# Full-row operands for the compressed attention products, retention norms in pairs of heads, and the last down-projection block ordered by token tiles

## The chip, the cores and the metric

The kernel runs on one core of one Trainium2 chip. The metric is the device time of one execution in microseconds (us); lower is better. Work is spread over TensorE (PE in the profile; its weight loads are PEld), VectorE (DVE), ScalarE (ACT), GpSimd (POOL) and the DMA queue of SyncE (SP).

## What is computed

Two post-norm layers over 512 tokens of width 1024. Each layer projects the tokens to a pooling mixer, six retention heads and six sparse-attention heads (two key/value groups of three heads), maps their outputs back with `w_out`, normalizes, and runs a gated MLP of width 2816 with a causal convolution, then a second layer norm. The parts that matter here, cut from the reference:

```python
def _retention(q, k, v, g, gn_g, pos):          # 6 heads of 64
    ...
    o = (inner + cross).reshape(b, t, h, dh)
    mu = jnp.mean(o, axis=-1, keepdims=True)
    var = jnp.mean(jnp.square(o - mu), axis=-1, keepdims=True)
    on = ((o - mu) * lax.rsqrt(var + GN_EPS)).reshape(b, t, RET_WIDTH) * gn_g
    return (jax.nn.silu(g.astype(f32)) * on).astype(q.dtype)

def _compress(kv, pos_emb, w1, b1, w2):         # 31 blocks of 32 tokens, stride 16
    ...
    return jax.nn.gelu(flat @ w1 + b1) @ w2

    # in _nsa: scores, softmax and values over the 31 compressed blocks
    s_c = jnp.einsum('btgrd,bngd->bgrtn', qg, kc)
    p_c = _masked_softmax(s_c, ends[None, :] <= tq[:, None])
    o_cmp = jnp.einsum('bgrtn,bngd->btgrd', p_c, vc)

    # per layer
    x = _layernorm(DEEPNORM_ALPHA * x + mix, ln1_g[l], ln1_b[l])
    f = _conv_ffn(x, ffn_w_gate[l], ffn_w_up[l], ffn_conv_w[l], ffn_conv_b[l], ffn_w_down[l])
    x = _layernorm(DEEPNORM_ALPHA * x + f, ln2_g[l], ln2_b[l])
```

## The kernel before

Tokens are four tiles t of 128 (`NT`). float32 products are made from float32r parts: every operand is split into a rounded half and the rest (`hi_lo`: a copy on ACT, a subtraction on DVE), and `mm3` issues three matmuls, hi*hi, hi*lo and lo*hi. Where the left operand holds both halves side by side (`vcs`, `VS`, `VR`: 64 columns of hi and 64 of lo), one matmul per half of the right operand is issued and the two column halves are added afterwards.

The order of the work is not written by hand. `Plan.record` collects every instruction with its dependencies and a price (`price`); `Plan.schedule`, a list scheduler with one queue for each engine, picks by rank among instructions that are ready in its model, and also decides which buffers are given out. PSUM has eight banks with limits for each use (`BANKS`: at most 3 for "mm", 4 for "tr", 5 for "s", 1 for "pv"); 29 scratch tiles "u", 14 weight tiles "w" (`NW`, one 128x1024 half each) and 5 raw weight tiles. On each engine the issued order is then fixed. All instructions are recorded at line 424, so the trace is read by tiles.

In each layer: the retention stage (`retention`, with the projections, pooling, `fill_cmp_*` and `fill_kcs` as filler), the attention stage (`attention`: `scores` and `values` for each token tile i and group g, with the output projection and the first norm, `fill_out1`, as filler), then the MLP (`ff_plain`, `ff_seven`) and its down-projection.

- `retention`: for each head h, `o_part` accumulates [128, 512] in one "pv" bank, adds its halves into `otr` [64, 512] (ACT copy, DVE add); `n_part` transposes `otr` in four pieces of 64 rows, norms the head with DVE, ACT and a POOL `pow`, and writes half of `YB`; after every second head `t_part` transposes `YB` into `mixT`.
- The compressed branch: `fill_cmp_mlp` leaves `ab` (66 rows), which `fill_cmp_act` transposes; `fill_cmp_out` makes `kd` (64 rows) and `vcs` (32 rows); `fill_kcs` transposes `kd`. In `values(i, g)` the job with b == 2 is the compressed one: the probabilities `pc` [128, 3, 32] are transposed to 32 rows, split into `PT`, and multiplied with `vcs`, two matmuls of 32 rows and 384 columns among those of `VS` with 128 rows.
- The down-projection runs in blocks of features (`BLOCKS`, the last one of 6). `ffn_order` lists ("w", block, half h of 512 columns) and ("down", block, h, t). In the last block h = 0 comes first for all t (tiles 0 to 2 together in three banks, all but the last feature first), then the weights of h = 1, then h = 1 for each t. A token tile is normed (`layernorm`) right after its h = 1 part. In the last layer the norm has form "m" (`LAST_NORM`): ACT and POOL take columns 704 to 1024 (`SHARE`), DVE the rest; then SP stores the tile. In the first layer the tile is transposed for layer 2.

Of the kernel before, what the change touches and what calls it, by code (L numbers as in the profile page):

```python
# [426 lines left out]
def trunk(tc, x_d, pos_d, w_in, w_out, w_gate, w_up, w_down, cst_d, prm_d,  # L427
# [4 lines left out]
    with es:  # L432
# [424 lines left out]
        prm = C([P, L, Q_N], F, "prm")  # L857
        for l in range(L):
# [113 lines left out]
            vcs = C([32, 2, P], R, "vcs", 1)  # L972
# [21 lines left out]
            def fill_cmp_mlp(i):  # L994

                ch, cl = state.pop(("CT", i))
                W = take(2)
                q = ps("mm", [P, 512])[0:66, 0:256].rearrange("p (a n) -> p a n", a=2)
                for t in range(8):
                    w = W[t // 4]  # L1000
                    mm3(q, (ch[:, t], cl[:, t]), (w[:, 0, :, t % 4], w[:, 1, :, t % 4]), t == 0, t == 7)
                ab = Q([66, 2, P], F, "ab", 1)
                nc.scalar.copy(ab, q)
                state["ab", i] = ab
                yield

            def fill_cmp_act(i):
                ab = state.pop(("ab", i))
# [4 lines left out]
                nc.scalar.copy(hs, pt)  # L1013
# [15 lines left out]
            def fill_cmp_out(i):  # L1029
                ht = state.pop(("ch", i))  # L1030
                q2 = ps("mm", [P, 512])[0:64, 0:64]
                mm3(q2, (ht[:, 0], ht[:, 1]), (w2[:, 0, i], w2[:, 1, i]), True, True)
                if i == 0:
                    kd = state["kd"] = Q([64, 2, 64], F, "kd", 1)
                    rope(q2.unsqueeze(1), 64, 1, cos[0:64, NT], nsin[0:64, NT], [kd[:, 0:1]])
                    nc.gpsimd.tensor_copy(kd[:, 1], kd[:, 0])
                else:
                    for g in range(2):
                        nc.scalar.copy(vcs[:, g, 0:64], q2[32 * g:32 * g + 32])
                        nc.vector.tensor_tensor(vcs[:, g, 64:128], q2[32 * g:32 * g + 32], vcs[:, g, 0:64].bitcast(F), OP.subtract)  # L1040
                yield

            def fill_kcs():
                kd = state.pop("kd")
# [16 lines left out]
            def retention():  # L1061
# [49 lines left out]
                def n_part(h, tmp):  # L1111
                    p, e = h // 2, h % 2
# [5 lines left out]
                    m = small([P, 4, NT])  # L1118
                    ors = cst[:, K_ORS + h:K_ORS + 24:6].unsqueeze(2).to_broadcast([P, NT, 64])
                    nc.vector.tensor_tensor(a, pn, ors, OP.mult)  # L1120
                    nc.vector.tensor_reduce(m[:, 0], a, AX.X, OP.add)
                    nc.vector.tensor_scalar(m[:, 0], m[:, 0], 1.0 / 64, None, OP.mult)
                    nc.vector.tensor_tensor(a, a, m[:, 0].unsqueeze(2).to_broadcast([P, NT, 64]), OP.subtract)
# [3 lines left out]
                    nc.gpsimd.tensor_tensor(m[:, 2], m[:, 1], mhalf[:, 0:NT], OP.pow)  # L1127
                    nc.vector.tensor_tensor(a, a, m[:, 2].unsqueeze(2).to_broadcast([P, NT, 64]), OP.mult)
                    if e == 0:
                        cache["yb"] = U([P, NT, 2, 64], n="YB")  # L1130
                    yb = cache["yb"]
                    engine(WHO[3]).tensor_tensor(yb[:, :, e], a, VG[p][:, 1, :, 64 * e:64 * e + 64], OP.mult)
                    if e:
                        return yb
# [13 lines left out]
                def back():  # L1148
# [5 lines left out]
                    if tmp is not None:  # L1154
                        later.append((n_part, h, tmp))

                def norm():
                    f, h, tmp = later.pop(0)
                    yb = f(h, tmp)
                    if yb is not None:  # L1160
                        later.append((t_part, h // 2, yb))
# [94 lines left out]
            def values(i, g):  # L1256
# [13 lines left out]
                for at, (b, j) in enumerate(jobs):  # L1270
# [4 lines left out]
                    PT = U([P, 2, 3, P], R, n="PT")  # L1275
                    hi_lo(PT[0:n, 0], PT[0:n, 1], pt[0:n])
# [37 lines left out]
            def layernorm(t, y, g, b, how, cuts=(0, 512, D)):  # L1314
# [7 lines left out]
                if how in "am":  # L1322
                    nc.vector.scalar_tensor_tensor(mv[:, 4:5], mv[:, 0:1], -1.0, mv[:, 3:4], OP.mult, OP.mult)
                for lo, hi, who in ((SHARE, D, "a"), (0, 512, "v"), (512, SHARE, "v")) if how == "m" else ((0, 512, how), (512, D, how)):
# [58 lines left out]
            if l == 0:  # L1383
                masks()
            one, mask = masked
# [111 lines left out]
            xT2 = None  # L1497
            if PLAIN:
# [10 lines left out]
            for what, *of in ffn_order:  # L1509
                if what == "seven":  # L1510
                    ff_seven(of[0])
                elif what == "w":
# [6 lines left out]
                    wd = take(-(-nb // 2))  # L1519
                elif what == "down":  # L1520
# [3 lines left out]
                    if lastb and h == 0 and t < 3:  # L1524

                        if t == 0:
                            qs = [ps("mm", [P, 512]) for _ in range(3)]
                            for ks in (range(nb - 1), (nb - 1,)):
                                for i in range(3):
                                    sum_down(qs[i], wd, b0, nb, i, ks)  # L1530
                            for i in range(3):
                                add_down(qs[i], ib, i, 0, 512)
                        continue
                    for lo, hi in ((0, 256), (256, 512)) if end else ((0, 512),):
                        q = ps("mm", [P, hi - lo])
                        sum_down(q, wd, b0, nb, t, range(nb), lo, hi)
# [83 lines left out]
NORM1, NORM2, LAST_NORM = "maav", "vvvv", "mmmm"  # L1620
SHARE = 704
# [55 lines left out]
```

## Time and profile before

| | us |
|---|---|
| median of 3 runs | 1276.33 (1276.01 to 1276.76) |
| the profiled execution | 1275.91 |
| its span | 1274.1 |
| PE busy | 1256.3 (99%) |
| PE weight loads busy | 1126.1 (88%) |
| DVE busy | 1027.2 (81%) |
| ACT busy | 705.3 (55%) |
| POOL busy | 339.4 (27%) |

The span is the time between the first and the last recorded instruction; the 1.8 us between it and the execution's time lie around it. A matmul's recorded duration is modelled and overlaps its neighbours' (a 512-column matmul is given 0.39 us while the next one starts 0.23 us later), so PE's cost is read from starts, not from durations.

### The profile page before, as it was taken

To read this page: it belongs to the slowest core of one execution; us is meant where nothing else is said; L and a number is where in the kernel's file an instruction comes from. 1 tells how busy PE (TensorE), PEld (TensorE's weight loads), DVE (VectorE), ACT (ScalarE), POOL (GpSimd) and SP (SyncE) were. 2 spreads that over 40 slices of the span, in tenths; PEclk is the share of its full clock that TensorE was granted. 3 is DMA by queue.
4 is the path that set the end of the run, shared out by engine and by line. 5 is a ranking of instruction groups with operands and counts; after the bars stand their busy time and mean duration, and the time that the engine had idled before them with its cause. 6 is when DMAs were issued, how large, how long until landed. Compare 5 with 4: busy or idle time off the path is not lost.

```text
span 1274.1 us, 21523 instructions
## 1 busy us (share of the span) xinstructions
PE 1256.3 (99%) x8044; PEld 1126.1 (88%) x8044; DVE 1027.2 (81%) x1957; ACT 705.3 (55%) x1459; POOL 339.4 (27%) x256
## 2 busy tenths in 40 slices
PE   9999999999999999999999999999999999999996
PEld 6789898889999999999888898888899999999995
DVE  7868888697888988888786687777887888888876
ACT  5445567665555555555334455865764555655540
POOL 1132303333322322212122322133513223222023
PEclk9999999999999999999999999999999999999998
DMA  8331513101433433345342215221023333434321
GB/s 273 117 85 32 168 68 119 48 1 34 120 105 99 120 91 108 109 125 154 122 141 83 67 50 182 80 71 34 18 77 90 95 106 99 122 102 126 100 67 67
DMA packets 142601, 123.24 MB, mean 97 GB/s; under 512 B 6688, under 2 KB 116000, under 8 KB 142496
## 3 DMA queue, kind: packets, MB, share of 16 engines
q1 hardware_dynamic: 142496, 121.86, 31.7%
q8 instruction: 63, 1.03, 0.3%
q14 instruction: 42, 0.34, 0.1%
HBM read 117.65 MB, written 4.19 MB: 96 GB/s over the span
## 4 chain that ended last, share of the span: by engine, by line
PE 94%; DVE 3%; ACT 2%; issue 0%; POOL 0%; POOLq 0%; DVEq 0%; ACTq 0%
PE mm L424 47%; PE s L424 39%; PE tr L424 5%; PE pv L424 3%; DVE y L424 1%; ACT P L424 1%; ACT PT L424 0%; DVE w L424 0%; DVE xq L424 0%; ACT y L424 0%; ACT xq L424 0%; DVE ps L424 0%; POOL y L424 0%; ACT xf L424 0%; DVE sm L424 0%
## 5 line engine op out<-in xcount | busy, mean ns | idle before, releaser
L424 POOL TENSOR_TENSOR w<-raw,w 128x1024 fp32r<-128x1024 f32 (+3 forms) x116 | 232.1, 2003 | 630.1 <-ACT w L424 355.7
L424 ACT CAST w<-raw 128x512 fp32r<-128x512 f32 (+2 forms) x403 | 290.7, 742 | 196.7 <-PE s L424 123.2
L424 DVE TENSOR_TENSOR w<-raw,w 128x512 fp32r<-128x512 f32 (+3 forms) x288 | 234.0, 831 | 41.2 <-ACT w L424 36.1
L424 PE MATMUL mm<-w,hT 128*128 128x512 f32 (+1 forms) x1074 | 262.3, 391 | 0.0
L424 PE MATMUL s<-xq,w 128*128 128x256 f32 x1944 | 251.1, 281 | 0.2
L424 PEld LDWEIGHTS s<-xq,w 128*128 128x128 f32 x1944 | 243.1, 189 | 6.2 <-DVE xq L424 0.6
L424 PE MATMUL mm<-w,xT 128*128 128x512 f32 (+3 forms) x1152 | 239.9, 353 | 1.8 <-DVE w L424 1.5
L424 PE MATMUL s<-xs,w 128*128 128x256 f32 x1824 | 234.0, 281 | 0.0
L424 PEld LDWEIGHTS s<-xs,w 128*128 128x128 f32 x1824 | 226.0, 189 | 2.3
L424 PEld LDWEIGHTS mm<-w,hT 128*128 128x128 f32 x1074 | 193.6, 188 | 37.5
L424 PEld LDWEIGHTS mm<-w,xT 128*128 128x128 f32 x1152 | 190.1, 188 | 27.1 <-ACT xT L424 1.7
L424 DVE TENSOR_TENSOR raw<-raw,raw 128x512 f32<-128x512 f32 (+1 forms) x114 | 100.3, 880 | 6.4 <-DMA raw<-in_w_up 4.8
L424 DVE TENSOR_TENSOR y<-y,mm 128x512 f32<-128x512 f32 (+1 forms) x97 | 63.2, 673 | 22.4 <-PE mm L424 21.9
L424 ACT COPY pq<-s 128x256 f32<-128x256 f32 x152 | 55.2, 368 | 43.0 <-PE s L424 42.7
L424 PE MATMUL mm<-w,mixT 128*128 128x512 f32 x240 | 74.5, 415 | 1.1 <-DVE OM L424 1.1
L424 DVE SCALAR_TENSOR_TENSOR pq<-gu,prm,pq 128x511 f32<-128x511 f32 x76 | 66.7, 877 | 3.5 <-ACT pq L424 3.2
L424 POOL TENSOR_TENSOR sm<-sm,mhalf 128x1 f32<-128x1 f32 (+1 forms) x28 | 26.5, 947 | 123.5 <-DVE sm L424 123.5
L424 DVE TENSOR_TENSOR gu<-s,pq 128x256 f32<-128x256 f32 x76 | 30.8, 418 | 29.2 <-PE s L424 25.0
L424 DVE TENSOR_TENSOR PT<-tr,PT 128x384 fp32r<-128x384 f32 (+1 forms) x96 | 48.9, 543 | 6.6 <-ACT PT L424 5.8
L424 ACT ACTIVATE P<-s,sm 128x128 f32<-128x128 f32 (+3 forms) x96 | 49.3, 533 | 8.1 <-DVE sm L424 7.8
L424 ACT CAST PT<-tr 128x384 fp32r<-128x384 f32 (+1 forms) x96 | 42.0, 482 | 19.7 <-PE tr L424 19.1
L424 POOL TENSOR_SCALAR P<-P,sm 128x384 f32<-128x384 f32 (+3 forms) x40 | 24.4, 624 | 104.0 <-DVE sm L424 66.0
(195 smaller groups left out, 1699.9 us busy)
## 6 DMA issues: line engine op xcount, KB each, us to landing
raw<-in_w_gate SPq DMA_DIRECT2D x76, 256.0 KB, 3.5
raw<-in_w_up SPq DMA_DIRECT2D x76, 256.0 KB, 3.8
raw<-in_w_down SPq DMA_DIRECT2D x36, 512.0 KB, 3.8
raw<-in_w_in SPq DMA_DIRECT2D x32, 512.0 KB, 4.3
raw<-in_w_out SPq DMA_DIRECT2D x14, 512.0 KB, 4.0
raw<-in_w_in SPq DMA_DIRECT2D x8, 530.0 KB, 4.3
raw<-in_w_down SPq DMA_DIRECT2D x16, 256.0 KB, 2.8
raw<-in_w_in SPq DMA_DIRECT2D x8, 384.0 KB, 3.2
```

Source lines behind the costliest of these rows:

```text
L424: getattr(getattr(self.nc, op.engine), op.method)(*a, **k)
```

## The change

Four edits:

1. `vcs`, `ab`, `kd` and two new tiles `ptc[g]` become constant tiles of 128 rows, zeroed once in `zeros()` (three ACT copies and three POOL memsets in the first layer). `vcs` holds its 32 rows twice; `ptc` holds the hi half of the transposed probabilities in rows 0 to 31 and the rest in rows 32 to 63. The compressed product of one (i, g) is one matmul over 128 rows. The transposes of `ab` and `kd` take 128 rows.
2. `o_part` writes two heads into one `otr` tile of 128 rows, `n_part` runs once for each pair: four transposes of 128 rows, and DVE, ACT and POOL instructions of 512 instead of 256 columns.
3. In the last block of the down-projection both weight halves are taken first; then (t, h) runs (0,0), (1,0), (0,1) together, then (1,1), (2,0), (2,1), (3,0), (3,1). A tile is normed after its h = 1 part.
4. The norm of the very last tile has form "e": as "m", with the columns from 832 (`LAST_SHARE`) for ACT and POOL.

The diff, cut to its core:

```diff
-            for h in range(2):
-                down.append(("w", b0, nb, h))
-                down.extend(("down", ib, b0, nb, h, t) for t in range(NT))
+            if b0 + nb < NFF:
+                for h in range(2):
+                    down.append(("w", b0, nb, h))
+                    down.extend(("down", ib, b0, nb, h, t) for t in range(NT))
+            else:
+                down.extend(("w", b0, nb, h) for h in range(2))
+                down.extend(("down", ib, b0, nb, h, t) for t, h in ((0, 0), (1, 0), (0, 1), (1, 1), (2, 0), (2, 1), (3, 0), (3, 1)))
...
+        vcs = C([P, 2, P], R, "vcs")
+        ptc = [C([P, 3, P], R, f"ptc{g}") for g in range(2)]
+        ab = C([P, 2, P], F, "ab")
+        kd = C([P, 2, 64], F, "kd")
+        def zeros():
+            z = U([P, 2 * P], n="z")
+            nc.gpsimd.memset(z, 0.0)
+            nc.scalar.copy(vcs, z.rearrange("p (a n) -> p a n", a=2))
+            for g in range(2):
+                nc.scalar.copy(ptc[g], z[:, 0:P].unsqueeze(1).to_broadcast([P, 3, P]))
+            nc.gpsimd.memset(ab, 0.0)
+            nc.gpsimd.memset(kd, 0.0)
...
-                pt = ps("tr", [P, 2, 66])
+                pt = ps("tr", [P, 2, P])
                 for a in range(2):
-                    tr(pt[:, a], ab[:, a], 66)
+                    tr(pt[:, a], ab[:, a])
...
+                    nc.scalar.copy(vcs[32:64], vcs[0:32].bitcast(F))
...
-                pt = ps("tr", [P, 64])
-                tr(pt, kd.rearrange("p a d -> p (a d)"), 64)
+                pt = ps("tr", [P, P])
+                tr(pt, kd.rearrange("p a d -> p (a d)"))
...
-                        tmp = U([64, 2, S], n="otr")
-                        nc.scalar.copy(tmp[:, 0], o[64:128])
-                        nc.vector.tensor_tensor(tmp[:, 1], o[0:64], tmp[:, 0], OP.add)
-                        return tmp
+                        e = h % 2
+                        if e == 0:
+                            cache["ot"] = U([P, 2, S], n="otr")
+                        tmp = cache["ot"]
+                        nc.scalar.copy(tmp[0:64, 0], o[64:128])
+                        nc.vector.tensor_tensor(tmp[64 * e:64 * e + 64, 1], o[0:64], tmp[0:64, 0], OP.add)
+                        return tmp if e else None
...
-                    pn = ps("tr", [P, NT, 64])
+                    pn = ps("tr", [P, NT, 2, 64])
                     for t in range(NT):
-                        tr(pn[:, t], tmp[:, 1, t * P:(t + 1) * P], 64)
-                    on = U([P, 2, NT, 64], n="on")
+                        tr(pn[:, t].rearrange("p e d -> p (e d)"), tmp[:, 1, t * P:(t + 1) * P])
+                    on = U([P, 2, NT, 2, 64], n="on")
...
+                    if n < P:
+                        mm(o, lhs, PT, first, last)
+                        return
                     mm(o, lhs, PT[0:n, 0], first, False)
                     mm(o, lhs, PT[0:n, 1], False, last)
...
-                    PT = U([P, 2, 3, P], R, n="PT")
-                    hi_lo(PT[0:n, 0], PT[0:n, 1], pt[0:n])
+                    if n < P:
+                        PT = ptc[g]
+                        hi_lo(PT[0:n], PT[n:2 * n], pt[0:n])
...
-                    if lastb and h == 0 and t < 3:
+                    early = ((0, 0), (1, 0), (0, 1))
+                    if lastb and (t, h) in early:
...
-NORM1, NORM2, LAST_NORM = "maav", "vvvv", "mmmm"
-SHARE = 704
+NORM1, NORM2, LAST_NORM = "maav", "vvvv", "mmme"
+SHARE, LAST_SHARE = 704, 832
```

## Rows read from the trace of the kernel before

**Rows 1.** Page: busy time by engine, and the chain that ended last by engine.

```profile
PE 1256.3 (99%) x8044; PEld 1126.1 (88%) x8044; DVE 1027.2 (81%) x1957; ACT 705.3 (55%) x1459; POOL 339.4 (27%) x256
...
PE 94%; DVE 3%; ACT 2%; issue 0%; POOL 0%; POOLq 0%; DVEq 0%; ACTq 0%
```

**Rows 2.** By stretch: length, busy us of PE, PEld, DVE, ACT, POOL, clock, DMA.

```profile
176.00:302.00 126.00, 124.14 (x736) 106.14 (x735) 97.68 (x219) 84.84 (x200) 44.95 (x42) 1.00 0.17 51
1266.00:1270.00 4.00, 0.00 (x0) 0.00 (x0) 2.66 (x5) 0.65 (x1) 2.88 (x5) 0.51 0.42 165
...
256.00:276.00 20.00, 20.00 (x114) 16.55 (x113) 18.88 (x43) 11.04 (x27) 5.29 (x7) 1.00 0.01 2
```

**Rows 3.** Timeline of PE, 128-row matmuls and transposes: start, us, what, shapes, count.

```profile
173.89 0.68 PE L424 MATMUL mm<-w,xT 128*128 128x384 f32 x3
...
607.61 21.79 PE L424 MATMUL mm<-w,hT 128*128 128x512 f32 x93
...
98.13 0.60 PE L424 MATMUL tr<-ident,YB 128*128 128x128 f32 x4
98.49 0.48 PE L424 MATMUL mm<-w,xT 128*128 128x256 f32 x2
```

**Rows 4.** Timeline of PE around one pair of compressed products, first layer.

```profile
245.07 0.95 PE L424 MATMUL mm<-w,mixT 128*128 128x512 f32 x3
245.94 0.43 PE L424 MATMUL pv<-PT,vcs 32*128 32x384 f32 x1
246.31 0.49 PE L424 MATMUL mm<-w,mixT 128*128 128x512 f32 x1
246.73 0.44 PE L424 MATMUL pv<-PT,vcs 32*128 32x384 f32 x1
247.10 0.51 PE L424 MATMUL mm<-w,mixT 128*128 128x512 f32 x1
```

**Rows 5.** Timeline of PE around another pair, back to back, first layer.

```profile
277.88 0.59 PE L424 MATMUL pv<-PT,VS 128*128 128x384 f32 x2
278.40 1.00 PE L424 MATMUL pv<-PT,vcs 32*128 32x384 f32 x2
279.33 0.44 PE L424 MATMUL pv<-PT,VS 128*128 128x384 f32 x1
```

**Rows 6.** Timeline of PE around the 64-row transposes of one retention head.

```profile
69.03 0.40 PE L424 MATMUL mm<-w,xT 128*128 128x512 f32 x1
69.36 0.46 PE L424 MATMUL tr<-ident,otr 64*128 64x64 f32 x4
69.75 0.39 PE L424 MATMUL s<-QTr,KSr 128*128 128x256 f32 x1
```

**Rows 7.** Chain that ended last, end of the attention stage, first layer.

```profile
273.08 1.51 ACT PT L424 x4
```

**Rows 8.** Groups by shape of DVE, a retention norm step: count, busy, mean ns, idle before.

```profile
L424 DVE TENSOR_TENSOR on<-on,sm 128x256 f32<-128x256 f32 x24 | 10.5, 437 | 1.0 <-POOL sm L424 0.8
```

**Rows 9.** Timeline of the end: last matmuls, norms of tiles 2 and 3.

```profile
1231.51 30.91 PE L424 MATMUL mm<-w,hT 128*128 128x512 f32 x150
...
1262.45 0.42 DVE L424 TENSOR_TENSOR y<-y,mm 128x256 f32<-128x256 f32 x1 [0.21 <-PE mm L424]
1262.79 0.15 DVE L424 TENSOR_SCALAR sm<-sm 128x1 f32<-128x1 f32 x1
...
1263.52 0.42 DVE L424 BATCH_NORM_STATS2 sm<-y 128x6 f32<-128x256 f32 x1
...
1264.36 0.65 ACT L424 ACTIVATE y<-y,sm 128x320 f32<-128x320 f32 x1 [4.74 <-DVE sm L424]
...
1268.88 0.94 POOL L424 TENSOR_TENSOR y<-y,lng 128x320 f32<-128x320 f32 x1 [0.96 <-ACT y L424]
1269.89 0.86 POOL L424 TENSOR_TENSOR y<-y,lnb 128x320 f32<-128x320 f32 x1
```

**Rows 10.** Timeline: layer 2's weights and first products; weights of the last block.

```profile
616.66 1.05 ACT L424 CAST w<-raw 128x1024 fp32r<-128x1024 f32 x1 [4.23 <-PE mm L424]
...
637.97 1.32 PE L424 MATMUL mm<-w,xT 128*128 128x512 f32 x5
...
1223.94 8.03 POOL L424 TENSOR_TENSOR w<-raw,w 128x1024 fp32r<-128x1024 f32 x3 [37.45 <-ACT w L424]
```

More of the change, by code (lines that the diff above doesn't have):

```diff
@@ L1033, in fill_cmp_out @@
                 if i == 0:
-                    kd = state["kd"] = Q([64, 2, 64], F, "kd", 1)
-                    rope(q2.unsqueeze(1), 64, 1, cos[0:64, NT], nsin[0:64, NT], [kd[:, 0:1]])
-                    nc.gpsimd.tensor_copy(kd[:, 1], kd[:, 0])
+                    rope(q2.unsqueeze(1), 64, 1, cos[0:64, NT], nsin[0:64, NT], [kd[0:64, 0:1]])
+                    nc.gpsimd.tensor_copy(kd[0:64, 1], kd[0:64, 0])
                 else:
                     for g in range(2):
-                        nc.scalar.copy(vcs[:, g, 0:64], q2[32 * g:32 * g + 32])
-                        nc.vector.tensor_tensor(vcs[:, g, 64:128], q2[32 * g:32 * g + 32], vcs[:, g, 0:64].bitcast(F), OP.subtract)
+                        v = vcs[0:32, g]
+                        nc.scalar.copy(v[:, 0:64], q2[32 * g:32 * g + 32])
+                        nc.vector.tensor_tensor(v[:, 64:128], q2[32 * g:32 * g + 32], v[:, 0:64].bitcast(F), OP.subtract)
+                    nc.scalar.copy(vcs[32:64], vcs[0:32].bitcast(F))
                 yield
             def fill_kcs():
-                kd = state.pop("kd")
-                pt = ps("tr", [P, 64])
-                tr(pt, kd.rearrange("p a d -> p (a d)"), 64)
+                pt = ps("tr", [P, P])
+                tr(pt, kd.rearrange("p a d -> p (a d)"))
+                pt = pt[:, 0:64]
                 nc.scalar.copy(kcs, pt)
@@ L1126, in n_part @@
                     nc.vector.tensor_scalar(m[:, 1], m[:, 1], 1.0 / 64, EPS, OP.mult, OP.add)
[L1127 to L1134, printed above, removed]
+                    nc.gpsimd.tensor_tensor(m[:, 0].rearrange("p t e -> p (t e)"), m[:, 1].rearrange("p t e -> p (t e)"), mhalf, OP.pow)
+                    nc.vector.tensor_tensor(a, a, each(m[:, 0]), OP.mult)
+                    yb = U([P, NT, 2, 64], n="YB")
+                    engine(WHO[3]).tensor_tensor(yb.rearrange("p t e d -> p t (e d)"), a.rearrange("p t e d -> p t (e d)"), VG[p][:, 1], OP.mult)
+                    return yb
                 def t_part(p, yb):
@@ L1154, in back @@
                     if tmp is not None:
-                        later.append((n_part, h, tmp))
+                        later.append((n_part, h // 2, tmp))
                 def norm():
-                    f, h, tmp = later.pop(0)
-                    yb = f(h, tmp)
+                    f, p, tmp = later.pop(0)
+                    yb = f(p, tmp)
                     if yb is not None:
-                        later.append((t_part, h // 2, yb))
+                        later.append((t_part, p, yb))
                 nxt_h = heads(0)
@@ L1384, in trunk @@
                 masks()
+                zeros()
             one, mask = masked
@@ L1497, in trunk @@
             xT2 = None
+            wd = [None, None]
             if PLAIN:
@@ L1518, in trunk @@
                             x_src = nc.tile(dp, [S, D], F, "xs", nm("xs"), 1)
-                    wd = take(-(-nb // 2))
+                    wd[h] = take(-(-nb // 2))
                 elif what == "down":
@@ L1523, in trunk @@
                     end = lastb and h == 1 and t == NT - 1 and l == L - 1
-                    if lastb and h == 0 and t < 3:
-                        if t == 0:
-                            qs = [ps("mm", [P, 512]) for _ in range(3)]
+                    early = ((0, 0), (1, 0), (0, 1))
+                    if lastb and (t, h) in early:
+                        if (t, h) == early[0]:
+                            qs = [ps("mm", [P, 512]) for _ in early]
                             for ks in (range(nb - 1), (nb - 1,)):
[L1529 to L1534, printed above, removed]
+                                for q, (i, j) in zip(qs, early):
+                                    sum_down(q, wd[j], b0, nb, i, ks)
+                            for q, (i, j) in zip(qs, early):
+                                add_down(q, ib, i, 512 * j, 512 * j + 512)
+                        if h == 0:
+                            continue
+                        done = True
+                    else:
+                        done = False
+                    for lo, hi in () if done else ((0, 256), (256, 512)) if end else ((0, 512),):
                         q = ps("mm", [P, hi - lo])
-                        sum_down(q, wd, b0, nb, t, range(nb), lo, hi)
+                        sum_down(q, wd[h], b0, nb, t, range(nb), lo, hi)
                         add_down(q, ib, t, 512 * h + lo, 512 * h + hi)
```

28 lines of the change are left out of this document (14 added, 14 removed).

## Prediction

> **What bounds the kernel now.** I read the page first: PE is busy in 99% of the span and makes 94% of the chain that ended last [rows 1]. DVE is next with 81%. So time taken off PE's stream is time gained, unless PE then waits for another engine. Busy time by stretch comes next: in the first layer's attention stage PE is busy for 124.1 of 126.0 us, DVE for 97.7 and ACT for 84.8 [rows 2]; DVE has room there except in one stretch of 20 us, where it is busy for 18.9. [...]
>
> A recorded matmul duration overlaps the next one, so the price of a matmul is the distance of two starts. In a run of 93 full-row matmuls of 512 columns this is (21.79 - 0.39) / 92 = 0.233 us, in one of three with 384 columns (0.68 - 0.34) / 2 = 0.17 us; four full-row transposes and the step to the next matmul take 98.49 - 98.13 = 0.36 us [rows 3]. (The 0.39 and 0.34 are what one such matmul is recorded with.) Against these I hold the matmuls with fewer rows.
>
> **Part 1, compressed products.** The third matmul of the first row starts about 245.62 (two steps of 0.233 and one late step of 0.085 before it). The 32-row product starts at 245.94, so 0.32 after a step of 0.233: 0.09 lost going in. It takes 246.31 - 245.94 = 0.37 until the full-row matmul starts, instead of 0.17: 0.20 lost coming out. The second product loses 246.73 - 246.31 - 0.233 = 0.19 going in and 0.20 coming out [rows 3, 4]. Together 0.68 us, and as one of the two products disappears, 0.17 more: 0.85 us for this pair. Another pair stands back to back [rows 5]: 279.33 - 278.40 = 0.93 for both, 0.10 before them (278.40 minus the second start near 278.13, minus 0.17), 1.03 in all; one full-row product of 0.17 remains: 0.86, of which some is a wait. The least a pair loses, without any wait, is 2 x 0.20 + 2 x 0.09 + 0.17 = 0.75. I take 0.78, near the low end since waits stay. There are 16 pairs (two layers, four token tiles, two groups): 16 x 0.78 = 12.5 us, bounds 12.0 and 13.8.
>
> [...]
>
> What is new beside it: zeroing, three ACT copies and three POOL memsets once, and one ACT copy per layer to double `vcs`. None feeds PE soon; estimate, from the 0.65 us of a 320-column ACT instruction [rows 9], under 2 us of ACT in a stage where no product of `vcs` is due yet: nothing on the path; if that cover were gone, 2 us. `ptc[g]` is written again only after the other group and a whole token tile, so its new wait is long satisfied. The split of `PT` keeps its instructions and their columns.
>
> **Part 2, retention in pairs.** A head's four 64-row transposes come in at 69.36 - 69.03 = 0.33 after a 512-column matmul (0.10 over 0.233) and take 69.75 - 69.36 = 0.39 to the next one [rows 6]: 0.49, for a pair of heads 0.98. One pair of 128-row transposes is 0.36 [rows 3]. Saved: 0.62 x 6 pairs = 3.7 us; without waits in the 0.39 perhaps 3.1. The two transposes of `kd` lose a way in and out in the same manner, 0.2 each, 0.4 together. Those of `ab` (66 rows, 66 columns) become 128 columns wide: 8 of them, at most 0.11 each at the pace of full transposes (0.36 for four, less the short last step), I take +0.2; a gain there has no source.
>
> The norm's DVE steps become half as many of twice the length. A 256-column step has 0.437 us [rows 8]; two of them 0.87, one of 512 columns between 0.44 and 0.87. DVE cannot lose by it, and five such steps on six pairs give it up to 6 x 5 x 0.43 = 13 us, more likely half. That lies beside PE and counts nothing. What grows is a pair's latency, by at most five steps of 0.43 on DVE and as much again on ACT and POOL, some 3 to 4 us. `mixT` of the last pair is not needed before the attention stage's filler, so nobody on PE waits; what is queued behind on DVE is the splitting of scores, each behind one step longer by at most 0.43.
>
> **Does PE's gain arrive?** The compressed products lie in the attention stage. Near its end the chain leaves PE: ACT's `PT` copies carry 1.5 us at 273 [rows 7], inside the stretch in which DVE is also nearly full [rows 2]. A product saved there turns into a wait. These are the last token tile's two pairs in each layer: 4 x 0.78 = 3.1 us. I write off 2.5 (bounds 0 and 6, the latter if the tile before is caught too). PE: 12.5 + 3.7 + 0.4 - 0.2 - 2.5 = 13.9 us.
>
> **Parts 3 and 4, the end.** PE's last matmul ends at 1262.4 and the span at 1274.1. DVE adds the last product at 1262.45 and then still works on tile 2 (its variance at 1262.79), so that tile 3's statistics start only at 1263.52 and its last POOL step ends at 1269.89 + 0.86 = 1270.75; store and end take 3.35 [rows 9]. After the change tile 2 has its last product two products of 18 matmuls earlier, 2 x 18 x 0.233 = 8.4 us, and is done. Tile 3 alone: add to 1262.87, statistics (0.42) and their sum to about 1263.56; from a variance to ACT 1264.36 - 1262.79 = 1.57, so ACT at 1265.13. ACT on 192 instead of 320 columns: 0.65 becomes 0.54; the two POOL steps 0.94 and 0.86 become at most that and, shrunk by the columns, at least 0.56 and 0.52; I take 0.73 and 0.71. With three gaps of 0.07 the end is 1265.13 + 0.54 + 0.73 + 0.71 + 0.14 = 1267.25. Gain 3.5 us; bounds 2.8 (nothing shrinks) and 3.9. DVE's extra 128 columns fit in the same time.
>
> The new order needs the weights of h = 1 already for the third early product, 7 us after 1231.5. POOL finishes them at 1223.94 + 8.03 = 1231.97 now [rows 9, 10]: no wait. But both halves now hold 12 of 14 weight tiles until (3, 0) runs. Before, ACT began three of layer 2's first four units at 616.66, after (3, 0) freed them; PE needs them from 637.97 [rows 10]. After, (3, 0) starts about 2 x 4.2 us before that, and its first two features free a pair 1.4 us later, the others at 2.8 and 4.2. Each unit is then 1.05 on ACT and some 2.7 on POOL (8.03 / 3) at worst: the second unit at 637.97 - 8.4 + 1.4 + 3.8 = 634.8, the fourth 2.8 us after it, and it is wanted only 3 x 1.4 us after the first. Nothing on the path, by 3 us of cover for the second and 4.6 for the fourth. The earlier norms of layer 1 bring nothing, as PE runs from one layer into the next.
>
> **The sum.** 13.9 + 3.5 = 17.4 us. Against the profiled execution: span 1274.1 - 17.4 = 1256.7, with 1.8 around it 1258.5; the median of the runs lies 0.4 above that execution: 1258.9 us.
>
> **The rivals.**
> - All of PE's gain arrives (nothing written off): 1276.3 - 16.4 - 3.5 = 1256.4. For it: PE has filler in the attention stage. Against: [rows 7].
> - Zero rows do not help, only the count does: a full load costs as much as a short one. One of two products goes, half of 1.03 x 16 = 8.2 us; the transposes save 6 x 0.49 = 2.9, the end 3.5: 1261.7. Against: [rows 3].
> - The attention stage is bound by ACT and DVE for most of its length: a third of 12.5 arrives, 4.2, with 3.9 and 3.5: 1264.7. For it: DVE's 18.9 of 20. Against: 124.1 of 126 for PE.
> - Slower: at the layer boundary the held weight tiles come free late, and DVE makes the lower halves only after the norms of tiles 2 and 3. [...] It decides from a loss of 17.4 us: two norms of some 6 us each, three units of 2.3 on ACT and DVE one after the other are 19; time 1278. Against: the 3 us of cover above.
>
> **How the numbers follow.** Forecast 0.45, all arrives 0.24, zero rows do not help 0.08, attention bound elsewhere 0.17, slower 0.03; 0.03 are left for a schedule that is simply worse ordered, half of it within 0.2%. 0.2%, 2.6 us, is about what a measurement of this kernel can tell from no change. The range runs from the upper bounds of the parts (13.8 + 3.7 + 0.4 - 0.2 + 3.9 = 21.6, so 1254.7) to past the third rival: 1254.7 to 1265.5. Faster 0.95, same 0.02, slower 0.03.
>
> **What would show it.** Parts 1 and 2: in the new trace compressed products and `otr` transposes have 128 rows, the step behind a product is 0.17, four `otr` transposes take 0.36, and the second layer's MLP starts some 7 us earlier relative to its first products. If PE's idle time grows at the end of each attention stage, more was to be written off. Part 3: from the last matmul to the span's end some 8.2 us instead of 11.7. It would be wrong if full-row products also stood 0.37 apart, or PE stalled at the layer boundary.

## The result and the profile after

The changed kernel takes 1260.44 us (median of four runs, 1259.87 to 1262.72), the kernel before, beside it, 1276.17: a ratio of 0.9881, interval 0.9863 to 0.9898, or 15.7 us less. 17.4 us were forecast, from 1276.33 to 1258.9. Measured once more later (changed_again, below) it took 1260.14 against 1275.95. Single executions of one and the same kernel differ here by 1 to 3 us, which matters for the smaller questions below.

The first two lines are the page's busy times of the changed kernel, the answer to [rows 1]; the next two are two of the stretches of [rows 2] (start and end, length; busy us and instructions of PE, PEld, DVE, ACT and POOL; mean granted clock, DMA share).

```profile
PE 1238.4 (98%) x8004; PEld 1120.6 (89%) x8004; DVE 1030.6 (82%) x1915; ACT 704.3 (56%) x1458; POOL 336.8 (27%) x247
...
PE 92%; DVE 5%; ACT 1%; issue 1%; SPq 0%; DMA 0%; POOL 0%; POOLq 0%; DVEq 0%; ACTq 0%
...
176.00:302.00 126.00, 124.17 (x792) 110.87 (x791) 102.71 (x229) 85.90 (x208) 47.24 (x43) 1.00 0.17 51
256.00:276.00 20.00, 18.97 (x129) 16.66 (x128) 17.94 (x44) 15.71 (x36) 8.95 (x10) 1.00 0.01 2
```

PE still bounds the kernel, but DVE's share of the chain went from 3% to 5%: some steps on PE now wait for DVE. In the same 126 us of the attention stage PE issues 792 matmuls instead of 736. In the 20 us from 256 on, where PE had no idle time before, it now has 1.0; the work there is not the same, as the changed kernel is some 8 us ahead by then (a compressed product among output products starts at 237.80 below and at 245.94 in [rows 4]).

PE's timeline of the changed kernel around a compressed product among value products, around another among products of 512 columns, the one of layer 1 that waits longest, and around the transposes of a pair of retention heads; the answers to [rows 4] and [rows 6]:

```profile
192.68 0.50 PE L424 MATMUL pv<-PT,VS 128*128 128x384 f32 x2
193.02 0.34 PE L424 MATMUL pv<-ptc,vcs 128*128 128x384 f32 x1
193.20 0.34 PE L424 MATMUL pv<-PT,VS 128*128 128x384 f32 x1
...
237.80 0.34 PE L424 MATMUL pv<-ptc,vcs 128*128 128x384 f32 x1
237.97 0.39 PE L424 MATMUL mm<-w,mixT 128*128 128x512 f32 x1
...
269.56 0.41 PE L424 MATMUL pv<-ptc,vcs 128*128 128x384 f32 x1 [0.74 <-DVE ptc L424]
...
81.26 0.60 PE L424 MATMUL tr<-ident,otr 128*128 128x128 f32 x4
81.62 0.71 PE L424 MATMUL mm<-w,xT 128*128 128x512 f32 x2
```

The step behind a compressed product is 0.17 to 0.18 us where it was 0.37 (so in 10 of the 16; in the six that stand behind transposes it is 0.25 to 0.26), and four transposes for two heads take 0.36 where eight took 0.98 with their way in.

The end of the changed kernel, the answer to [rows 9]:

```profile
1224.82 25.05 PE L424 MATMUL mm<-w,hT 128*128 128x512 f32 x125
...
1249.91 0.42 DVE L424 TENSOR_TENSOR y<-y,mm 128x256 f32<-128x256 f32 x1 [1.24 <-PE mm L424]
1250.37 0.43 DVE L424 BATCH_NORM_STATS2 sm<-y 128x6 f32<-128x256 f32 x1
...
1252.55 0.55 ACT L424 ACTIVATE y<-y,sm 128x192 f32<-128x192 f32 x1 [7.27 <-DVE sm L424]
1253.17 0.91 POOL L424 TENSOR_TENSOR y<-y,lng 128x192 f32<-128x192 f32 x1 [0.85 <-ACT y L424]
1254.16 0.59 POOL L424 TENSOR_TENSOR y<-y,lnb 128x192 f32<-128x192 f32 x1
```

DVE waits for PE before the last addition, as tile 2 is out of the way, and the statistics follow at once. From PE's last matmul to the end of the span are 1258.1 - 1249.9 = 8.2 us, 11.7 before. So of the 16.0 us by which the span shrank, 3.5 belong to the end and 12.5 to PE's stream (1262.4 - 1249.9). In the repeat PE's stream gave 13.2.

Where along the stream it came is read from the first or last start of a kind of matmul, each against the same event of the kernel before (worked out from the starts of the matmuls; us earlier; "the MLP's sums" are the products that read `xs`):

| event | before, us | changed | changed, repeat | part 1 alone | part 2 alone |
|---|---|---|---|---|---|
| first scores of the attention stage, layer 1 | 167.6 | 2.0 | 1.4 | -1.7 | 2.4 |
| first product of the MLP's sums, layer 1 | 326.5 | 9.6 | 9.0 | 4.1 | 4.6 |
| last one, layer 1 | 602.8 | 7.7 | 8.3 | 3.5 | 0.8 |
| first product of layer 2 | 638.0 | 7.8 | 8.4 | 3.6 | 0.9 |
| first scores of the attention stage, layer 2 | 796.0 | 7.5 | 8.2 | 3.5 | 1.7 |
| first product of the MLP's sums, layer 2 | 952.7 | 12.2 | 12.9 | 9.3 | 1.5 |
| PE's last matmul | 1262.1 | 12.5 | 13.2 | 9.3 | 1.6 |

Each column is one profiled execution: part 1's took 1266.39, part 2's 1274.07, 1.1 and 1.4 above the medians below. Up to the MLP of layer 1 more arrives than was forecast for a layer; then up to 1.9 us are given back in a stage that the change does not touch, and layer 2's retention stage brings nothing, though its transposes got as much shorter. The forecast's sign for layer 2, an MLP some 7 us earlier relative to the layer's first products, came out smaller: 12.2 - 7.8 = 4.4 us, 4.5 in the repeat.

### The profile page after: what moved, and what is told of

Its sections match the earlier page's. It is cut to its first block, busy times and chain, and to the rows that moved or that the text cites. A ratio compares the mean times of both kernels' runs of the same rounds, so it can differ in the third digit from the quotient of the medians.

```text
span 1258.1 us, 21371 instructions
## 1 busy us (share of the span) xinstructions
PE 1238.4 (98%) x8004; PEld 1120.6 (89%) x8004; DVE 1030.6 (82%) x1915; ACT 704.3 (56%) x1458; POOL 336.8 (27%) x247
## 4 chain that ended last, share of the span: by engine, by line
PE 92%; DVE 5%; ACT 1%; issue 1%; SPq 0%; DMA 0%; POOL 0%; POOLq 0%; DVEq 0%; ACTq 0%
PE mm L424 46%; PE s L424 38%; PE tr L424 4%; PE pv L424 3%; DVE y L424 1%; DVE w L424 1%; DVE PT L424 1%; SPq L424 0%; DVE xq L424 0%; DMA raw<-in_w_up 0%; DVE VR L424 0%; DVE sm L424 0%; DVE rt L424 0%; ACT xq L424 0%; ACT xf L424 0%
## 5 line engine op out<-in xcount | busy, mean ns | idle before, releaser
L424 DVE TENSOR_REDUCE sm<-s 128x1 f32<-128x384 f32 (+4 forms) x88 | 43.1, 528 | 8.6 <-PE s L424 7.9
L424 PEld LDWEIGHTS mm<-w,mixT 128*128 128x128 f32 x240 | 42.5, 189 | 7.0 <-ACT P L424 0.2
L424 PE MATMUL pv<-PT,VS 128*128 128x384 f32 x160 | 48.0, 364 | 0.7 <-ACT P L424 0.4
```

Source lines behind the costliest of these rows:

```text
L424: getattr(getattr(self.nc, op.engine), op.method)(*a, **k)
```

## The experiments

**Each part alone.** The kernels are the kernel before with part 1, with part 2, with parts 3 and 4, and with part 3 without form "e" (`LAST_NORM` stays "mmmm").

> The kernel before with part 1 alone (compressed products over 128 rows, both halves in one; transposes of ab and kd over 128 rows). Theory (a short-row matmul breaks the overlap of weight load and matmul on both sides, and what is saved at the end of the attention stage turns into waits): 12.5 + 0.4 - 0.2 - 2.5 = 10.2 us less than before, about 1266.0. Rival, only the count of products matters: 8.2 less, 1268.0. Rival, the attention stage is bound by ACT and DVE: about 4 less, 1272. All of it arrives: 12.7 less, 1263.5.

Measured 1265.34 against 1275.82, ratio 0.9918 (0.9905 to 0.9932): 10.5 less, where the forecast's share for it was 10.2. The count of products alone (8.2 less, 1268.0) and a stage bound by ACT and DVE (4 less) lie outside the interval (8.7 to 12.1 less); so does an arrival of all 12.7. In the table the two attention stages bring 5.8 us each (4.1 + 1.7 and 9.3 - 3.5), 11.6 together, more than the 10.0 that the sum left them. Everything else loses 2.3 in that execution. About 1.2 of it are lost at the very beginning, where PE's granted clock is 0.50 from 8.0 to 11.4 us (the kernel before has 1.00 there): its first product starts at 8.12, 0.2 before the other's, its fourth at 11.25, 1.0 behind.

> The kernel before with part 2 alone (retention outputs and norms in pairs of heads). Theory: PE saves 0.62 us a pair, 3.7 us in all, nothing lost in the retention stage where PE hardly waits: about 1272.5. Rival, only the count matters: 2.9 less. Rival, the longer DVE steps and the later norm bring new waits: no change, 1276.

Measured 1272.68, ratio 0.9979 (0.9970 to 0.9988): 3.1 less (1.5 to 3.8): something arrives, but the time cannot tell the full 3.7 from the rival's 2.9. That the price of few rows is gone is read from the rows, 0.36 against 0.98. The table shows that this is not 1.8 in each layer: 4.6 us are gained up to layer 1's MLP and 3.9 of them lost in it. Its profile has the two waits named below, 2.1 us near 400 and 1.3 at 692, and behind the first a loss of another 1.5 us, by the clock:

```profile
401.00 1.99 PE L424 MATMUL mm<-w,hT 128*128 128x512 f32 x6 [1.88 <-ACT hT L424]
...
402.20:405.40 3.20, 3.20 (x12) 0.50 0.00 0
406.00:409.00 3.00, 3.00 (x28) 1.00 0.00 0
```

The last two lines are stretches with PE's busy time, its instructions, the mean granted clock and the DMA's share. In the first one PE's granted clock is 0.50, and its 512-column matmuls start 0.427 us apart instead of 0.233.

> The kernel before with parts 3 and 4 alone (last block by token tiles, form e for the last tile). Theory: PE's last matmul ends where it did, and the end behind it shrinks from 11.7 to 8.2 us: 3.5 less, about 1272.7. Rival, weights held longer stall PE at the layer boundary or at the third early product: the same 8.2 us at the end, but PE ends later by the stall.

Measured 1273.05, ratio 0.9979 (0.9970 to 0.9988): 2.8 less. In its profile PE's last matmul ends at 1262.2 and the span at 1270.3, 8.1 us; PE waits 0.6 us once at the beginning of layer 2, for a tile's norm, and nowhere at the third early product. The rival with the held weights falls.

> The kernel before with part 3 alone (order by token tiles; the last tile is normed in form m as before). Theory: the end shrinks by tile 2's work being out of the way, 2.8 us (the lower bound of the sum, where nothing shrinks), about 1273.4; form e is then worth 0.7 us. If the gain of the end came from form e, this one stays near 1276.

Measured 1273.18, ratio 0.9980 (0.9971 to 0.9988): 2.6 less. The end behind the last matmul is 1271.4 - 1262.9 = 8.5 us. The order shortens the end by 3.2 us, form "e" by another 0.4: as said, the order, but form "e" is worth less than the expectation's 0.7. That 0.7 is 3.5 less the bound of 2.8, and the bound was too low: by the forecast's own terms an end in which nothing shrinks is 1265.13 + 0.65 + 0.94 + 0.86 + 0.14 = 1267.72, a gain of 3.0, which leaves 0.5 for form "e". The steps above agree: ACT 0.55 instead of 0.65, the two POOL steps 0.91 + 0.59 = 1.50 instead of 0.94 + 0.86 = 1.80.

The parts alone add up to 10.5 + 3.1 + 2.8 = 16.4, together they give 15.7 or 15.8: they add within what the runs can tell.

**What a shape costs.** Four extra products in each feature tile of the MLP, where PE waits for nothing:

```diff
+                shapes = ((32, P), (64, P), (96, P), (P, P), (P, 32), (P, 64))
+                kr, kc = shapes[(f - PLAIN) % 6]
+                dum = ps("pv", [P, 384])
+
+                def probe(first, last):
+                    nc.tensor.matmul(dum[0:kc], vcs[0:kr, 0, 0:kc], ptc[0][0:kr], start=True, stop=True)
...
                 product(X, "11", "11")
+                probe(0, 0)
...
```

> The changed kernel with four extra products of 384 columns in each of the 38 feature tiles of the seven-product form of the MLP, between its products, into a PSUM bank that nobody reads; the shape of the left operand changes from feature tile to feature tile: 32, 64, 96 and 128 rows with 128 columns, then 128 rows with 32 and with 64 columns. It measures the price of a shape alone, in a stage where PE waits for nothing. Theory: 128 rows cost 0.17 us to the next start and nothing before; 32 and 64 rows cost 0.09 more going in and 0.20 more coming out; 96 rows as 128 (66 did in the kernel before). Fewer columns: no theory, 0.17 if only rows matter. Rival, a full-row load is as exposed as a short one: all shapes alike. The run as a whole: 152 products, some 25 to 45 us longer than the changed kernel.

It took 1305.74 us in one run, 45 longer. The other three extra products follow the next three products in the same way. PE's timeline, one extra product of five of the six kinds between products of 256 columns:

```profile
416.83 0.52 PE L424 MATMUL s<-xq,w 128*128 128x256 f32 x3
417.28 0.44 PE L424 MATMUL pv<-ptc,vcs 32*128 32x384 f32 x1
417.65 0.51 PE L424 MATMUL s<-xs,w 128*128 128x256 f32 x2
...
435.80 0.44 PE L424 MATMUL pv<-ptc,vcs 64*128 64x384 f32 x1
436.17 0.50 PE L424 MATMUL s<-xs,w 128*128 128x256 f32 x2
...
454.18 0.34 PE L424 MATMUL pv<-ptc,vcs 96*128 96x384 f32 x1
454.35 0.52 PE L424 MATMUL s<-xs,w 128*128 128x256 f32 x3
...
469.00 0.34 PE L424 MATMUL pv<-ptc,vcs 128*128 128x384 f32 x1
469.18 0.40 PE L424 MATMUL s<-xs,w 128*128 128x256 f32 x2
...
485.88 0.34 PE L424 MATMUL pv<-ptc,vcs 128*32 128x384 f32 x1
486.05 0.51 PE L424 MATMUL s<-xs,w 128*128 128x256 f32 x3
```

The distance to the next start is 0.37 us with 32 and 64 rows and 0.17 with 96 and 128 rows, and also 0.17 with 128 rows and only 32 columns. Over all of them (16 to 24 of a kind, worked out from the starts) the medians are:

```
rows x columns   step before   step behind
 32 x 128          0.209         0.368
 64 x 128          0.209         0.370
 96 x 128          0.117         0.179
128 x 128          0.118         0.176
128 x  32          0.117         0.175
128 x  64          0.120         0.176
```

A product of 32 or 64 rows costs 0.091 going in and 0.192 coming out, 0.283 us in all, in a stage without waits. The forecast's 0.09 and 0.20 from two pairs were right, and the rival by which a full-row load is as exposed as a short one is out. Fewer columns cost nothing here: 0.175 and 0.176 behind, where 128 have 0.176. The overlap that the expectations name can be read from the weight loads: in the kernel before, 29 of the 32 loads for a 32-row compressed product start within 0.002 us of their own matmul (245.94 for the first product of [rows 4]), and the full-row load behind that product, too, starts with its matmul, at 246.31; in the changed kernel the load for the product at 237.80 starts at 237.57, with the matmul before it, and the median of the 16 is 0.173 us ahead.

**Zero rows or count.** The compressed product with the zero rows left out, and issued twice:

```diff
-                        mm(o, lhs, PT, first, last)
+                        mm(o, lhs[0:64], PT[0:64], first, last)     # k64_half_rows
...
-                        mm(o, lhs, PT, first, last)
+                        mm(o, lhs, PT, first, False)                # two_full_products
+                        mm(o, lhs, PT, False, last)
```

> The changed kernel, but the compressed product reads only rows 0 to 63 of both operands (the zero rows are left out; the result is the same sum). Theory: a product of 64 rows breaks the overlap as the 64-row transposes did, 0.09 us going in and 0.10 to 0.20 coming out, 16 times 0.19 to 0.29: 3.0 to 4.6 us slower than the changed kernel, some 1264, less what the end of the attention stage hides. Rival, zero rows do not help and only the count of products does: the same as the changed kernel, 1260.4.

Measured 1266.98, ratio to before 0.9929 (0.9916 to 0.9943): 6.5 to 6.8 more than the changed kernel, from leaving out rows that hold only zeros; the order of the instructions is the same on every engine. 16 x 0.283 = 4.5 of it is the price of the shape; more than the 4.6 of the expectation's upper end was measured, and the rest is not in these products. In its profile the two attention stages lose 4.7 us against the changed kernel's (2.3 and 2.4) and the MLP of layer 1 loses 2.4: the wait near 396 us described below is 2.7 us long, 0.8 longer, and from 400.2 on PE's granted clock is 0.50 for a stretch, as in p2_pairs, which costs 1.5.

```profile
192.91 0.51 PE L424 MATMUL pv<-PT,VS 128*128 128x384 f32 x2
193.35 0.44 PE L424 MATMUL pv<-ptc,vcs 64*128 64x384 f32 x1
193.72 0.45 PE L424 MATMUL pv<-PT,VS 128*128 128x384 f32 x1
...
400.30:403.60 3.30, 3.30 (x14) 0.50 0.00 0
```

The first three lines are the same place as in the changed kernel above: the step behind the product is 0.37 instead of 0.18, the step before it 0.27 (from the second start, 0.17 after 192.91) instead of 0.17. The last line is a stretch as in p2_pairs.

> The changed kernel with the compressed product of 128 rows issued twice, so that the compressed part of the output is doubled: as many products as before the change, all over full rows. Theory: a full-row product costs 0.17 us, 16 more are 2.8 us: some 1263. Rival, a product costs 0.37 however many rows it has: 5.9 us, some 1266.

Measured 1263.45, ratio 0.9901 (0.9888 to 0.9915): 3.0 to 3.3 more than the changed kernel for 16 more products, 0.19 to 0.21 each; 2.8 were expected, and the rival's 5.9 lies outside its interval. In its profile the two stand 0.17 to 0.18 apart where they follow each other directly, 0.26 behind transposes. So of what a pair of compressed products gave, 0.17 to 0.2 comes from the missing product and the rest from the rows.

**Where the missing 1.5 us went.** In the changed kernel's profile PE waits in two places that the forecast did not have. This is the timeline of the first layer's MLP, then of the second layer's retention stage:

```profile
383.39 1.46 SPq L424 DMA_DIRECT2D w2r<-in_w2v  x1
...
392.26 1.23 DVE L424 TENSOR_TENSOR raw<-raw,raw 128x1024 f32<-128x1024 f32 x1 [2.89 <-DMA raw<-in_w_up]
393.35 1.29 POOL L424 TENSOR_TENSOR w<-raw,w 128x512 fp32r<-128x512 f32 x1 [4.27 <-DMA raw<-in_w_gate]
393.40 1.78 DVE L424 TENSOR_TENSOR pq<-gu 128x512 f32<-128x512 f32 x1
395.88 1.44 PE L424 MATMUL mm<-w,hT 128*128 128x512 f32 x5 [1.72 <-ACT hT L424]
...
684.90 2.63 POOL L424 TENSOR_TENSOR w<-raw,w 128x1060 fp32r<-128x1060 f32 x1 [5.01 <-ACT w L424]
685.08 3.00 DVE L424 TENSOR_TENSOR VR<-VG,VR 128x512 fp32r<-128x512 f32 x1
688.13 1.48 PE L424 MATMUL pv<-PTr,VR 128*128 128x512 f32 x8 [1.18 <-DVE VR L424]
```

The same steps in the kernel before:

```profile
400.80 1.23 DVE L424 TENSOR_TENSOR raw<-raw,raw 128x1024 f32<-128x1024 f32 x1 [2.04 <-DMA raw<-in_w_up]
401.95 0.68 DVE L424 TENSOR_TENSOR pq<-gu 128x512 f32<-128x512 f32 x1
402.65 1.80 POOL L424 TENSOR_TENSOR w<-raw,w 128x512 fp32r<-128x512 f32 x1 [4.17 <-DVE pq L424]
...
691.99 0.68 DVE L424 TENSOR_TENSOR VR<-VG,VR 128x512 fp32r<-128x512 f32 x1
692.01 2.99 POOL L424 TENSOR_TENSOR w<-raw,w 128x1060 fp32r<-128x1060 f32 x1 [5.03 <-ACT w L424]
```

A DVE step with two SBUF operands that starts while POOL works on SBUF takes 1.78 or 3.00 us instead of 0.68: it ends 0.55 us after POOL does (394.64 and 395.18, 687.53 and 688.08). This holds for more than the two: of the 38 steps `pq<-gu` in this profile nine start within a POOL step and take 1.27 to 2.87 us, the other 29 take 0.68 to 0.69; of the 95 additions `y<-y,mm` of the same size, whose second operand lies in PSUM, 38 start within a POOL step and all of these take 0.68 to 0.69. PE then waits 1.3 us for `VR`. In the kernel before the same two steps start 0.02 us apart with DVE's first, and POOL's is the longer one; POOL's comes first in every kernel with part 2 but the two that take the POOL step away (lo_on_dve, lo_on_dve_f9), and in none without it. Near 394 two things meet: `w_up` lands late, after one small transfer took SP 1.46 us to issue instead of the 0.43 of the kernel before, and POOL gets in ahead of DVE. In the kernel before the same steps stood at 402 with no wait of PE.

The wait near 394 can cost more than its length. In p2_pairs, k64_half_rows and lo_on_dve PE waits 2.1, 2.7 and 2.0 us there, and then its granted clock is 0.50 from 402.1, 400.2 and 398.4 on, before it is 1.00 again; each time the starts lose some 1.5 us against the usual steps. In the profiles of the changed kernel, two_full_products and lo_on_dve_f9 it waits 1.9, 2.1 and 2.2 us at the same place and the clock stays at 1.00 until after PE's last matmul.

The next kernels take the two waits apart. Each but changed_again is planned anew, and their orders differ from the changed kernel's in more than the step meant.

```diff
-LO_MIX, LO_FFN = "pvv", "p"
+LO_MIX, LO_FFN = "vvv", "p"        # lo_on_dve, lo_on_dve_f9
...
-                engine("v" if f >= NFF - 2 else SEVEN[name]).tensor_tensor(...)
+                engine("v" if f >= NFF - 2 or f == 9 else SEVEN[name]).tensor_tensor(...)    # lo_on_dve_f9
+                engine("v" if f >= NFF - 2 or f == 8 else SEVEN[name]).tensor_tensor(...)    # split_f8_on_dve, without the line above
...
-SLACK = {"tensor": 1.0, "vector": 1.1, "scalar": 1.05, "gpsimd": 1.2, "sync": 1.3, "wait": 1.6}
+SLACK = {"tensor": 1.0, "vector": 1.1, "scalar": 1.05, "gpsimd": 1.2, "sync": 1.3, "wait": 1.5}      # replan_wait
```

> The changed kernel, but the lower halves of the weights of the mixing stages are all made on DVE instead of one in three on POOL. In the changed kernel DVE's split of VR took 3.0 us at 685 instead of 0.68 while POOL worked on a weight, and PE waited 1.3 us. Theory (the shortfall comes from DVE and POOL steps that hold each other up in the newly planned order): that wait goes, 1 to 2 us less than the changed kernel, if DVE's extra 10 to 12 us in each mixing stage find room. Rival, DVE has no room there (80% busy): slower, up to 5 us.

Measured 1257.97 (1257.70 to 1260.84), ratio 0.9864 (0.9851 to 0.9877). The wait at `VR` is gone from its profile, as expected; three of its four runs lie near 1257.9, but its interval overlaps the changed kernel's, and its profiled execution, the slowest, took 1260.84. In that execution the clock is 0.50 from 398.4 on, as said above. Waits of 0.7 to 1.0 us appeared at the beginning of the first attention stage instead. That it is faster than the changed kernel is not shown, and lo_on_dve_f9 below, the same kernel but for one step, takes 1260.18.

> The changed kernel itself once more, beside the next two: 1260.4 and, if the waits found in its profile belong to its order and not to one execution, the same waits of about 1.9 us before a down-projection product near 394 us and 1.3 us at the VR split near 687 us.

1260.14 (1259.13 to 1261.77), ratio 0.9875 (0.9861 to 0.9890). The wait at `VR` is there again (1.3 us at 686): it belongs to the order. The one near 394 is not the same: the rows of DVE and POOL in this execution are

```profile
392.75 1.23 DVE L424 TENSOR_TENSOR raw<-raw,raw 128x1024 f32<-128x1024 f32 x1 [2.85 <-DMA raw<-in_w_up]
393.90 0.68 DVE L424 TENSOR_TENSOR pq<-gu 128x512 f32<-128x512 f32 x1
...
393.89 1.83 POOL L424 TENSOR_TENSOR w<-raw,w 128x512 fp32r<-128x512 f32 x1 [4.27 <-PE s L424]
```

and PE lost 0.7 us instead of 1.9. Here the two steps start 0.01 us apart; DVE's took 0.68, and POOL's was the longer one, 1.83 instead of 1.29. `w_up` came as late as before (DVE idle for 2.85 and 2.89), and the order is the same instruction by instruction, so the 1.1 us between the two waits go with DVE's step, and the 0.7 that stay with the transfer. This wait differs from execution to execution.

> The kernel with all lower halves of the mixing weights on DVE, and in addition one weight split of feature tile 9 on DVE instead of POOL (in both layers). That POOL step starts at 393 to 395 us, just ahead of a DVE step of 0.68 us that then takes 1.77, and PE waits about 2 us behind it. Theory: DVE is held up by the POOL step, 1.1 us of that wait goes; the other 0.9 us, a weight transfer that lands late, stays: 1257.0 against 1258.0. Rival, the late transfer alone sets the wait: nothing changes.

1260.18 (1258.75 to 1261.22), ratio 0.9874 (0.9859 to 0.9888); the wait near 396 stayed at 2.2 us. It tells nothing on the question: in its trace the POOL step that is missing is the one after the step meant, at 406; that at 395.5 is still there, and DVE's step behind it took 1.76.

> The changed kernel with one number of the planner's model changed (its allowance for waits 1.5 instead of 1.6), so that the same instructions come in another order. It measures what an order alone is worth. Theory (1 to 2 us of the change's shortfall are accidents of the new order): the time moves by up to 2 us either way, 1258.5 to 1262.5, with other waits in other places. Rival, the shortfall belongs to the change: within 0.5 us of the changed kernel, with the same waits.

1260.68 (1259.37 to 1261.25), ratio 0.9880 (0.9863 to 0.9896): within 0.6 us of the changed kernel. Some waits moved (1.2 us at 269, 1.3 at 744), some stayed (`VR` at 686), and PE's last matmul ends at 1249.5, between the changed kernel's two profiles (1249.9 and 1249.2). This is one other order; it moved less than the wide theory's 2 us, and it does not show what orders are worth in general.

> The changed kernel with one weight split of feature tile 8 on DVE instead of POOL (in both layers); the run that moved tile 9 had moved the step after the one meant, which stands at 393 to 395 us. Theory: the wait near 394 us has two parts, a weight transfer that lands late (0.5 to 0.8 us, different in each execution) and DVE's step of 0.68 us held up to 1.77 by the POOL step that starts just before it; without that POOL step the wait is at most 0.8 us and the median up to 1 us under the changed kernel's 1260.2. Rival, the transfer alone sets it: waits of up to 2 us remain in the profile and the median stays.

1258.93 (1258.55 to 1259.71), ratio 0.9867 (0.9851 to 0.9884). In its profile PE loses 0.4 us near 393 instead of 0.7 to 1.9, and the steps there are

```profile
392.01 1.23 DVE L424 TENSOR_TENSOR raw<-raw,raw 128x1024 f32<-128x1024 f32 x1 [1.48 <-DMA raw<-in_w_up]
393.16 0.68 DVE L424 TENSOR_TENSOR hT<-pq,hT 128x512 fp32r<-128x512 f32 x1
```

`w_up` is late again (DVE idle for 1.48), DVE's step behind it keeps its 0.68. But more changed than the POOL step: `pq<-gu` now stands ahead of `w_up`, at 387.74, where it took 2.47 behind another POOL step without a wait of PE. The median is 1.2 us under the repeat, about the expected 1, though the intervals overlap. That the wait near 394 has both sources, the larger one DVE held by POOL, rests on the two executions of the changed kernel above more than on this run.

## Why the prediction was right, and where it was off

- **The price of few rows** (0.09 in, 0.20 out, 0.17 for the product that disappears) held: 0.091 and 0.192 in the probe, 0.19 to 0.21 for a product in two_full_products. The time of the whole would not have shown it: 1260.4 is about as near to the rival in which zero rows do not help (1261.7) as to the forecast (1258.9). What decides are the steps in the rows and these two kinds of kernels. Part 1 alone gave 10.5 us where 12.5 + 0.4 - 0.2 - 2.5 = 10.2 stood in the sum. The zeroing cost nothing that can be seen: its ACT copies ran from 2.9 to 4.1 us, before PE's products began.
- **What was written off**, 2.5 us at the end of the attention stages, was right in place and too large. In both layers PE waits for the compressed product's operand behind the last token tile's transposes (0.9 us over the usual step, at 269 and 892, where 0.4 were lost before), and the wait for the last norm grew from 0.74 and 0.79 to 0.96 and 0.94. That is 1.4 us directly, and part 1 alone brought 11.6 of 12.5 us through its attention stages. So that 10.5 met 10.2 is in part luck: less was lost where the loss was expected, and more elsewhere. The reading of [rows 7], that the chain had left PE there, was the right sign.
- **Part 2** was sized at 3.7 and gave 3.1. Its PE term was right, 0.36 for four transposes. In its profiled execution two new waits, 2.1 and 1.3 us, and the low clock, 1.5, stand against it. What failed is the sentence that a longer DVE step delays those behind it by at most 0.43 us and nobody on PE waits: in the new order a DVE step with two SBUF operands fell behind a POOL step and was late by 2.3 us, at `VR`, and PE waited 1.3 for it. The forecast priced DVE's steps by their own length only. DVE's gain was also smaller than the "half of 13": the three kinds of steps on `on` went from 25.5 to 21.2 us, 4.3 in all.
- **The end**: 8.2 us forecast and 8.2 measured, though two terms were off in opposite directions (the first POOL step 0.18 longer, the second 0.12 shorter than assumed). The sum says three gaps of 0.07 and adds two; two is what the rows show. In the kernel with parts 3 and 4 alone the end is 3.6 us shorter, and the median time 2.8 (1.5 to 3.8).
- **The layer boundary**: weights held longer cost nothing. The wait of 0.6 us at 637, for a tile's norm, comes with part 3, where the sum had nothing: it is in p34_tail and p3_order too, and not in the kernel before, p1_compressed or p2_pairs. The clock stays at 1.00 there, and the wait is 0.6 us where the rival on the slower side had 19, so that rival had no part in it; a granted clock of 0.50 behind a wait showed in three other kernels near 400 us.
- **The missing 1.5 us** of 17.4 are in PE's stream, 12.5 (13.2 in the repeat) for 13.9. Against it stand 1.3 us at `VR`, 0.7 to 1.9 near 394 and 0.6 at 637, 2.6 to 3.8 us that the sum did not have. That less is missing is luck in the sense that errors of both signs met. By the table the retention stages brought 1.7 us (2.0 and -0.3) where 3.7 + 0.4 - 0.2 = 3.9 were forecast, the attention stages 12.3 (7.6 and 4.7) where 12.5 - 2.5 = 10.0 were, and everything else -1.5 where the sum had nothing; in the repeat 1.2, 12.3 and -0.3. The 9.6 us up to the MLP of layer 1 were not traced to single steps: part 2 alone is 4.6 us ahead there, with some 1.8 from its transposes, and waits that the kernel before had in that stretch (1.2 us at 194.5) are gone. Which of the new steps removed them stays open.

## What to carry to other kernels

In this stream of full-row matmuls, one with 32 or 64 rows cost 0.46 us where a full one costs 0.18, so the distance of two starts around odd shapes is worth reading before anything else; filling the rows with zeros was cheap, as the tiles are zeroed once. Although PE was busy for 99% of the span, of the 16.4 us that the forecast took off its stream 12.5 to 13.2 arrived: a total that fits is worth splitting by stages before it is believed. And the cover of a DVE step with two SBUF operands is not its own length only: a POOL step on SBUF that starts before it and still runs counts too (1.27 to 2.87 us instead of 0.68 for `pq<-gu`, 3.00 for `VR`). Last, a wait of PE of 2 to 2.7 us was followed in three profiles by a stretch at a granted clock of 0.50, another 1.5 us, so the granted clock belongs beside every list of waits.

## What the runs showed of the hardware that had not been expected

- The loss goes by rows in two classes: 32 and 64 rows cost 0.283 us more, 96 and 128 rows nothing, 32 or 64 columns nothing (probe_shapes). 66 rows cost nothing either in the kernel before (its transposes of `ab` go in after the usual 0.23 us and out after 0.03), so these needed no change.
- PE's granted clock fell to 0.50 in the middle of its stream, after waits of 2.1, 2.7 and 2.0 us (p2_pairs, k64_half_rows, lo_on_dve), and cost some 1.5 us each time; after waits of 1.9 to 2.2 us in three other profiles it did not.
- POOL's `pow` grows with the columns: 0.85 us for one column, 1.07 for four, 2.06 for eight (means of 16 and 12 in the kernel before, of 6 in the changed one). Two heads in one step saved nothing on POOL there.
- SP took 1.4 to 1.9 us to issue one small transfer in layer 1's MLP among others of 0.42 to 0.60, in ten of the fourteen profiles, not always the same transfer; in the kernel before, p1_compressed, p34_tail and p3_order the longest was 0.96. What holds it is open.
